# Attention on pairs of heads: VectorE and ScalarE work issued in written order by time behind each visit, and softmax transposes mostly in two PSUM banks of their own

## The chip, the core and the metric

The kernel runs on one NeuronCore of one Trainium2 chip. The metric is device time in microseconds (us) of one execution. The kernel before took 1141.73 us (median of 3 runs, 1139.65 to 1144.34). Its profiled execution took 1142.61 us, of which the span from the first to the last instruction is 1140.8 us.

The engines are named as the profile names them: PE is TensorE's matmul row and PEld its weight loads, DVE is VectorE, ACT is ScalarE, POOL is GpSimd, and SP is the engine that issues most transfers. L414 is line 414 of the kernel before.

## The reference

One layer on 1024 tokens of width 1024. Only the first third matters here:

```python
hn = rmsnorm(h, norm_mix_g[i])
z = hn @ w_in[i]                       # 512 columns for pooling, then q, k, v of 8 heads of 64
...
o = chunk_attention(q, k, v, rel_bias[i])
h = h + jnp.concatenate([a, o], axis=-1) @ w_out[i]
```

Attention works on chunks of 64 tokens; each sees itself and the 8 chunks before it, with a bias by clipped distance per head. A gated MLP with a causal convolution and a gated embedding follow; the change doesn't touch them.

## The kernel before, in words

Every product is made of three matmuls on a high and a low part of each operand (`mm3`, L136: high by high, high by low, low by high). So each matrix that enters a product is split first: ScalarE copies it to the rounded high part, and VectorE subtracts that from the source to give the low part (`split`, L142; ScalarE's half is L143, VectorE's L144).

**The attention stage** (L311 to L644) walks over 28 visits, `u` = 0 to 27, and a closing visit 28. The four groups of seven visits belong to the four pairs of heads. A visit takes one pair of heads and one tile of 128 query tokens (t = 2 to 7; the first visit of a pair takes t = 0 and 1 together). TensorE runs in the order in which the code is written. In a visit it does, in this order:

1. `probs_t(u-1)` (L380): transposes the finished softmax of the visit before, 64x64 blocks, up to 10 key tiles for the two heads, 20 matmuls (L395).
2. `scores(u)` (L357): the scores of this visit, 12 matmuls with up to 320 columns (L370), into PSUM banks 4 to 7, columns 0 to 320. The even banks belong to the first head, the odd ones to the second.
3. Filler: steps of a generator `rest()` (L587), which holds the projections for the other pairs of heads: q and k of pairs 1 and 2, the second half of v, q and k of pair 3, then the pooling columns. One step (a fill) is three matmuls of 512 columns, or six of 256 for v. A table (`fill_room`, L89) says how many fills each visit gets, 168 in all. The accumulating banks are 0 and 1 in turn, 8 fills to a bank (4 for v).
4. `values(u-1)` (L418), in every second visit: probabilities times v, 8 to 24 matmuls (L433, L434), into that one of banks 0 and 1 that isn't accumulating.

VectorE and ScalarE serve this. **Softmax** (L339): VectorE adds the bias and takes the row extreme (the reduction, L343 and L347), ScalarE exponentiates (L348), VectorE takes the reciprocal (L349), and the scaling is done by VectorE for the first head (L353) and by ScalarE for the second (L351). **Probabilities** (`probs_out`, L408): ScalarE copies the transposes out as high part (L413), VectorE forms the low part (L414). **Outputs**: ScalarE and VectorE fold the two halves of the output (L439, L440). **Banks**: a finished projection is taken out by VectorE (`qk_out` L279, `u_out` L517) or by both engines (`v_out` L274, L275). **Weights**: the next block of weights is loaded by SP and split (L454, L143, L144). **Lay**: q and k of the next pair are split (`lay`, L283). **Bias**: the table of the next heads is loaded and turned in sign by ScalarE (`load_bias`, L332, L335).

On these two engines a scheduler chose the order before: the code gives softmax, probabilities, outputs and bank clearing a raised priority (`tc.high_priority(AHEAD)`), and what is ready by the scheduler's reckoning is put in. The transposes of a visit with four or five key tiles lie in banks 4 to 7 from column 320 (key tiles 0 to 2 of each head) and in banks 2 and 3 (the rest), so that each head needs two copies per engine.

Of the kernel before, what the change touches and what calls it, by code (L numbers as in the profile page):

```python
# [64 lines left out]
FILL = 168  # L65
BASE = 6.0
# [14 lines left out]


def window_keys(u):

    t = UNITS[u][1][-1] if 0 <= u < NU else 0
    return min(t + 1, 6) if t % 2 else 0


def fill_room():  # L89


    vec_t, pe_t = [], []
    for u in range(NU):
        vec_t.append(BASE + 0.2 * (key_tiles(u) + key_tiles(u - 1)) + 0.25 * window_keys(u - 1))
        pe_t.append(0.4 + 0.18 * key_tiles(u) + 0.11 * key_tiles(u - 1) + 0.48 * window_keys(u - 1))
    lo, hi = 0.0, 10.0
    for _ in range(60):
        m = (lo + hi) / 2
        room = [max(0.0, m * v - p) / 0.68 for v, p in zip(vec_t, pe_t)]
        lo, hi = (m, hi) if sum(room) < FILL else (lo, m)  # L100
    return room


def trunk(tc, xT, pT, vecs, w_qk0, w_in, w_v, bias, counts, pool_w, w_out, w_up, w_down,
# [4 lines left out]
    with tc.tile_pool(name="sb", bufs=1) as sb, \  # L109
# [159 lines left out]
        def v_out(t, half, ps):  # L269
# [4 lines left out]
            act.activation(hi, pv, AF.Copy, scale=s)  # L274
            dve.scalar_tensor_tensor(lo, pv, s, rv(hi), ALU.mult, ALU.subtract)  # L275
# [5 lines left out]
        laid = set()  # L281

        def lay(c, x, h):  # L283

            laid.add((c, x, h))
            z = slice(h * 512, (h + 1) * 512)
            src = qk32[x][:, z]
            if x:
                hi, lo = [a[:, z] for a in K[c % 2]]
                return [lambda: act.activation(hi, src, AF.Copy),  # L290
                        lambda: dve.tensor_tensor(lo, src, rv(hi), ALU.subtract)]
            hi, lo = [a[:, z] for a in Q]
            return [lambda: act.activation(hi, src, AF.Copy, scale=-0.125),
                    lambda: dve.scalar_tensor_tensor(lo, src, -0.125, rv(hi), ALU.mult, ALU.subtract)]
# [37 lines left out]
        def load_bias(h):  # L332
            b = biasb[h % 3]
            sp.dma_start(b, bias[h])
            act.activation(b, b, AF.Copy, scale=-1.0)  # L335
            pool.memset(b[0:64, 576:640], BIG)
            pool.memset(b[64:128, 0:64], BIG)

        def softmax(x, b, ps, S, s_):  # L339

            n = S.shape[-1]
            if len(ps.shape) == 3:
                dve.tensor_tensor_reduce(  # L343
                    S.rearrange("p (a b) -> p a b", a=2), ps,
                    b.rearrange("p (a b) -> p a b", a=2), 1.0, BIG, ALU.add, ALU.min, s_[:, 0:1])
            else:
                dve.tensor_tensor_reduce(S, ps, b, 1.0, BIG, ALU.add, ALU.min, s_[:, 0:1])  # L347
            act.activation(S, S, AF.Exp, bias=s_[:, 0:1], scale=-1.0, accum_out=s_[:, 1:2])  # L348
            dve.reciprocal(s_[:, 2:3], s_[:, 1:2])  # L349
            if x:  # L350
                act.activation(S, S, AF.Copy, scale=s_[:, 2:3])  # L351
            else:
                dve.tensor_scalar(S, S, s_[:, 2:3], None, ALU.mult)  # L353
# [26 lines left out]
        def probs_t(u):  # L380
# [4 lines left out]
            def place(x, m):  # L385
                if total < 4:
                    return (6, 320 + HD * m) if x else (2, HD * m)
                return (4 + 2 * x, 320 + HD * m) if m < 3 else (2, P * x + HD * (m - 3))

            todo = []  # L390
            for x in range(2):
# [6 lines left out]
                for t in ts:  # L398
                    nk = min(t + 1, BANDT)
                    i0 = max(0, t - 4) - (t // 2 * 2 - 4)  # L400
                    parts = [(0, nk)] if total < 4 else [(0, 3), (3, nk)]
                    for a, b in parts:
                        bank, col = place(x, m + a)
                        todo.append((x, t % 2 * P, i0 + a, i0 + b, PS[:, bank:bank + 2, col:col + HD * (b - a)]))
# [3 lines left out]
        def probs_out(todo):  # L408
            for x, q, a, b, ps in todo:
                src = ps.rearrange("p a (k q) -> p a k q", q=HD)  # L410
                hi, lo = [PT[x][:, y, a:b, q:q + P].rearrange("p k (a q) -> p a k q", a=2) for y in range(2)]
                with tc.high_priority(AHEAD):
                    act.activation(hi, src, AF.Copy)  # L413
                    dve.tensor_tensor(lo, src, rv(hi), ALU.subtract)  # L414

        credit = 0.0

        def values(u):  # L418
# [5 lines left out]
            while c_ >= 2 and len(v_ready) < 2 * w + 2 or u < NU - 1 and at[0] < 2.0:  # L424
                next(fill)
                credit -= 1
            ks = list(range(max(0, 2 * w - 4), 2 * w + 2))
            for j in range(2):
                pt = PT[j]
                O = PS[:, (bankn[0] + 1) % 2, 256 * j:256 * j + 256]  # L430
                for n_, k in enumerate(ks):
                    idx = k - (2 * w - 4)
                    pe.matmul(O, V[:, k, 2 * c_ + j], pt[:, 0, idx], start=n_ == 0, stop=False)  # L433
                    pe.matmul(O, V[:, k, 2 * c_ + j], pt[:, 1, idx], start=False, stop=n_ == len(ks) - 1)  # L434
            for j in range(2):
                O = PS[:, (bankn[0] + 1) % 2, 256 * j:256 * j + 256]
                a, c = halves[j], halves[1 - j]
                with tc.high_priority(AHEAD):
                    act.activation(otmp[a], O[c], AF.Copy)  # L439
                    dve.tensor_tensor(o32[a, c_, w * 256:(w + 1) * 256], O[a], otmp[a], ALU.add)  # L440

# [6 lines left out]
        wvr = []  # L448

        def v_weights(z):  # L450
            for k in (slice(0, 2), slice(2, 4)):
                split(wvr[z][:, k], wv2[z][0][:, k], wv2[z][1][:, k])

        def weights(ct):  # L454
# [10 lines left out]
            for ks in (slice(0, 4), slice(4, 8)):  # L465
                split(t[:, ks], hi[:, ks], lo[:, ks])

        def project(ct, evac, wait=None):
            weights(ct)
            hi, lo = ready[ct]  # L470
            behind = blocks_[blocks_.index(ct) + 1] if ct != blocks_[-1] else None
            for h in range(2):
                bankn[0] += 1
                bank = bankn[0] % 2
                for k in range(KT):
# [906 lines left out]
```

## Time and profile before

| what | value |
|---|---|
| profiled execution | 1142.61 us |
| span of that execution | 1140.8 us |
| median of 3 runs | 1141.73 us |
| PE busy | 1120.6 us, 98% of the span |
| DVE busy | 866.2 us, 76% |
| ACT busy | 591.0 us, 52% |
| mean granted TensorE clock | 0.996 |

In a table of windows the first number of a cell is busy time in that stretch and the number in brackets counts instructions; PEclk is the granted clock. In a table of waits a row says who waited for whom, then the total, the number of times, and the longest. In a timeline the first number is the start in the span, the second the duration, and square brackets hold the idle time just ahead and what ended it. In a table of groups the numbers behind the bar are the total busy time and the mean of one in nanoseconds.

### The profile page before, as it was taken

The page shows a single profiled execution, that of the slowest core. Times are in us where ns is not written, and L with a number is a line of the kernel's source. Part 1 is how long each engine was busy: PE and PEld are TensorE (multiplying, and loading weights), DVE is VectorE, ACT ScalarE, POOL GpSimd, SP SyncE. Part 2 cuts the span into 40 slices and gives each one's busy share as a digit, 9 for nine tenths or more (in the row PEclk, how much of TensorE's full clock was granted, in tenths as well). Part 3 has the DMA queues.
Part 4 walks back from the last instruction along what each step waited for, and adds up shares of the span by engine and source line. Part 5 has one row for each costly group of instructions (what it writes and reads, how often), then busy time and mean ns, then how long its engine had stood idle before and what let it go on. Part 6 is the DMA issues. An engine that isn't in the chain of part 4 may idle for free.

```text
span 1140.8 us, 16198 instructions
## 1 busy us (share of the span) xinstructions
PE 1120.6 (98%) x5914; PEld 936.7 (82%) x5914; DVE 866.2 (76%) x1532; ACT 591.0 (52%) x1076; POOL 142.6 (12%) x188
## 2 busy tenths in 40 slices
PE   9999999999999999999999999999999999999997
PEld 7987888878788888888888888888888888888887
DVE  8576658678747887787787888787877789986845
ACT  8466667664744554444434444444444445564634
POOL 0000000056003200030102110211021102000000
PEclk9999999999999999999999999999999999999999
DMA  8101001105600055476557655765576556520003
GB/s 280 41 32 56 25 24 56 31 20 181 193 15 19 23 156 164 121 161 160 141 148 153 154 156 148 154 153 155 147 154 153 155 148 121 157 93 19 1 29 119
DMA packets 64879, 125.91 MB, mean 110 GB/s; under 512 B 7328, under 2 KB 8736, under 8 KB 64800
## 3 DMA queue, kind: packets, MB, share of 16 engines
q1 hardware_dynamic: 50688, 99.38, 26.8%
q0 software_dynamic: 13824, 25.17, 13.9%
q8 instruction: 46, 0.75, 0.3%
q14 instruction: 33, 0.27, 0.1%
q10 hardware_dynamic: 288, 0.33, 0.1%
HBM read 110.18 MB, written 14.68 MB: 109 GB/s over the span
## 4 chain that ended last, share of the span: by engine, by line
PE 83%; DVE 8%; ACT 5%; issue 2%; DMA 1%; POOL 1%; DVEq 0%; POOLq 0%; ACTq 0%; SPq 0%
PE PS L138 26%; PE PS L139 26%; PE PS L140 25%; DVE R L144 2%; PE PS L434 1%; PE PS L433 1%; ACT F L348 1%; ACT R L143 1%; PE PS L370 1%; DVE F L343 1%; ACT B L413 1%; DMA F<-in_w_out 1%; PE PS L395 1%; DVE B L414 1%; DVE F L440 1%
## 5 line engine op out<-in xcount | busy, mean ns | idle before, releaser
L138 PE MATMUL PS<-R 128*128 128x512 f32 (+1 forms) x1104 | 425.7, 386 | 1.7 <-ACT F L858 0.6
L139 PE MATMUL PS<-R 128*128 128x512 f32 (+1 forms) x1104 | 422.4, 383 | 0.0
L140 PE MATMUL PS<-R 128*128 128x512 f32 (+1 forms) x1104 | 422.2, 382 | 0.0
L138 PEld LDWEIGHTS PS<-R 128*128 128x128 f32 x1104 | 208.0, 188 | 45.1 <-ACT F L858 1.8
L140 PEld LDWEIGHTS PS<-R 128*128 128x128 f32 x1104 | 207.9, 188 | 40.5
L139 PEld LDWEIGHTS PS<-R 128*128 128x128 f32 x1104 | 208.1, 188 | 40.2 <-DVE R L248 1.3
L143 ACT ACTIVATE R<-F 128x512 fp32r<-128x512 f32 (+2 forms) x235 | 146.8, 636 | 179.6 <-PE PS L139 87.0
L144 DVE TENSOR_TENSOR R<-F,R 128x512 fp32r<-128x512 f32 (+2 forms) x235 | 162.7, 703 | 45.6 <-ACT R L143 42.4
L771 DVE TENSOR_TENSOR F<-F 128x512 f32<-128x512 f32 x88 | 60.5, 688 | 49.4 <-DMA F<-in_w_up 48.1
L1081 DVE TENSOR_TENSOR F<-F,PS 128x512 f32<-128x512 f32 x140 | 92.5, 681 | 6.2 <-PE PS L140 6.0
L143 ACT ACTIVATE BQ<-RW 128x512 fp32r<-128x512 f32 x90 | 52.6, 622 | 77.3 <-PE PS L139 73.3
L1024 POOL DMA_DIRECT2D RW<-Yd x56 | 49.5, 884 | 262.4 <-DMA RW<-Yd 199.1
L1024 POOL DMA_DIRECT2D RW<-in_w_down x40 | 36.1, 950 | 230.6 <-DMA RW<-in_w_down 194.0
L144 DVE TENSOR_TENSOR BQ<-RW,BQ 128x512 fp32r<-128x512 f32 x90 | 59.1, 685 | 2.5 <-PE PS L139 1.3
L414 DVE TENSOR_TENSOR B<-PS,B 128x384 fp32r<-128x384 f32 (+2 forms) x104 | 45.8, 460 | 15.8 <-ACT B L413 15.0
L348 ACT ACTIVATE F<-F,small 128x640 f32<-128x640 f32 (+4 forms) x64 | 44.3, 693 | 23.0 <-DVE small L343 20.0
L139 PE MATMUL PS<-BQ 128*128 128x512 f32 x140 | 54.6, 390 | 0.1
L140 PE MATMUL PS<-BQ 128*128 128x512 f32 x140 | 54.5, 390 | 0.0
L139 PE MATMUL PS<-R,BQ 128*128 128x512 f32 x140 | 54.5, 390 | 0.0
L138 PE MATMUL PS<-BQ 128*128 128x512 f32 x140 | 54.5, 389 | 0.0
L140 PE MATMUL PS<-R,BQ 128*128 128x512 f32 x140 | 54.5, 389 | 0.0
L138 PE MATMUL PS<-R,BQ 128*128 128x512 f32 x140 | 54.5, 389 | 0.0
(175 smaller groups left out, 1683.5 us busy)
## 6 DMA issues: line engine op xcount, KB each, us to landing
F<-in_w_up SPq DMA_DIRECT2D x91, 256.0 KB, 4.2
RW<-Yd SPq DMA_DIRECT2D x60, 256.0 KB, 3.7
RW<-Yd POOLq DMA_DIRECT2D x56, 256.0 KB, 5.0
RW<-in_w_down SPq DMA_DIRECT2D x50, 256.0 KB, 2.9
RW<-in_w_down POOLq DMA_DIRECT2D x40, 256.0 KB, 6.1
Yd<-F SPq DMA_DIRECT2D x40, 256.0 KB, 3.5
F<-in_w_in SPq DMA_DIRECT2D x10, 512.0 KB, 3.5
F<-in_xT SPq DMA_DIRECT2D x16, 256.0 KB, 5.8
```

The lines of the kernel that those rows point to most:

```text
L138: pe.matmul(ps, ahi, bhi, start=first, stop=False, skip_group_check=more)
L139: pe.matmul(ps, ahi, blo, start=False, stop=False, skip_group_check=more)
L140: pe.matmul(ps, alo, bhi, start=False, stop=last, skip_group_check=more)
L143: both = (act.activation(hi, src, AF.Copy), dve.tensor_tensor(lo, src, rv(hi), ALU.subtract))
L144: dve.tensor_tensor(lo, src, rv(hi), ALU.subtract))
L343: dve.tensor_tensor_reduce(S.rearrange("p (a b) -> p a b", a=2), ps, b.rearrange("p (a b) -> p a b", a=2), 1.0, BIG, ALU.add, ALU.min, s_[ ...
L348: act.activation(S, S, AF.Exp, bias=s_[:, 0:1], scale=-1.0, accum_out=s_[:, 1:2])
L370: pe.matmul(PS[:, places[x][y], 0:wide], q[halves[x], t * P:(t + 1) * P], k[halves[x], ki + y * wide:ki + (y + 1) * wide], start=i == 0, s ...
L414: dve.tensor_tensor(lo, src, rv(hi), ALU.subtract)
L771: return dve.tensor_tensor(rawu[to], rawu[a], rawu[b], op)
L1024: pool.dma_start(t, src, accum_op=ALU.add)
L1081: dve.tensor_tensor(t, t, PS[:, 4 + d], ALU.subtract if n in (1, 5) else ALU.add)
```

## The change

Three things change, and no arithmetic.

1. **Order on VectorE and ScalarE.** In the 29 visits both engines now run in written order. Each piece of work is pushed with a time in us behind the start of the visit (`push`), and `flush` writes out all that is pending in the order of these times. A flush comes ahead of `values`, at the end of the visit's fills, and where a bank or weights that are still pending are needed. The bias table is turned at the end of the seventh and of the second visit of a pair, not where it is loaded.
2. **Fill.** `fill_room` goes; a row of seven numbers (`ROOM`) serves each pair. `project_v` gives control back once ahead of its first matmul, and the visit's loop ends when the generator does so.
3. **Banks.** The transposes of both heads are numbered in one row; the first eight go to banks 2 and 3, the ninth and tenth to banks 6 and 7 from column 384.

```diff
-FILL = 168
-BASE = 6.0
+ROOM = (5.5, 5.5, 6, 5.5, 7, 5.5, 7)
+STEP = 0.68
...
+        pending, now, owed = [], [0.0], set()
+
+        def push(t, *fns):
+            for n, fn in enumerate(fns):
+                pending.append((t + 0.8 * n, len(pending), fn))
+
+        def flush():
+            todo = sorted(pending, key=lambda p: p[:2])
+            pending.clear()
+            owed.clear()
+            for _, _, fn in todo:
+                fn()
...
+                push(1.0 + 0.8 * z, least)
+                push(1.9 + 0.85 * z, lambda S=S, s_=s_: act.activation(
+                    S, S, AF.Exp, bias=s_[:, 0:1], scale=-1.0, accum_out=s_[:, 1:2]))
+                push(3.4 + 0.35 * z, lambda s_=s_: dve.reciprocal(s_[:, 2:3], s_[:, 1:2]))
+                push(3.9 + 0.1 * z, scaled)
...
             def place(x, m):
-                if total < 4:
-                    return (6, 320 + HD * m) if x else (2, HD * m)
-                return (4 + 2 * x, 320 + HD * m) if m < 3 else (2, P * x + HD * (m - 3))
+                n = total * x + m
+                return (2, HD * n) if n < 8 else (6, 384 + HD * (n - 8))
...
-                with tc.high_priority(AHEAD):
-                    act.activation(hi, src, AF.Copy)
-                    dve.tensor_tensor(lo, src, rv(hi), ALU.subtract)
+                push(0.9 if bank > 3 else 0.3 * n, lambda hi=hi, src=src: act.activation(hi, src, AF.Copy))
+                push(2.6 + 0.3 * n, lambda lo=lo, src=src, hi=hi: dve.tensor_tensor(lo, src, rv(hi), ALU.subtract))
+                n += bank < 4
...
-            while c_ >= 2 and len(v_ready) < 2 * w + 2 or u < NU - 1 and at[0] < 2.0:
+            while c_ >= 2 and len(v_ready) < 2 * w + 2 or u < NU - 1 and at[0] < 1.3:
                 next(fill)
                 credit -= 1
+                now[0] += STEP
+            flush()
...
+        def split_later(ct, parts):
+            t = max(5.2, now[0] + 0.4)
+            for i, (src, hi, lo) in enumerate(parts):
...
+                push(t + 0.7 * i, lambda src=src, hi=hi: act.activation(hi, src, AF.Copy), low)
...
         def project(ct, evac, wait=None):
             weights(ct)
+            if ct not in there:
+                flush()
...
         def project_v():
             v_weights(1)
+            yield False
+            flush()
...
                 def evac(h, ps, x=x):
-                    qk_out(x, h, ps)
+                    push(now[0] + 0.2, lambda: qk_out(x, h, ps))
...
                 lay_due(u)
-                credit += room[u]
-                while credit >= 1 and next(fill, True) is not False:
+                credit += ROOM[u % PER]
+                now[0] = 1.25
+                while credit >= 1:
+                    now[0] += STEP
                     credit -= 1
+                    if next(fill, True) is False:
+                        break
                     lay_due(u)
...
+            flush()
+            if u:
+                values(u - 1)
+            if turns and (u % PER == PER - 1 or u % PER == 1):
+                turns.pop(0)()
+            run_later(LATER)
...
+        with tc.manual_schedule(engines={mybir.EngineType.Activation, mybir.EngineType.DVE}):
+            for u in range(NU + 1):
+                unit(u)
```

How the rows of the built programs move is shown at three places. Lines of the changed kernel have other numbers; what they are is said each time.

**Place 1: PE at visit 11** (second pair, t = 5). Before, the row with 20 transposes (L395) and the 12 scores (L370) is followed by the fills of v (L138 to L140):

```order
L434 MATMUL PS<-B,R 128x256
L395 MATMUL PS<-ident,F 128x64 x20
L370 MATMUL PS<-R 128x320 x12
L138 MATMUL PS<-B,R 128x256
L139 MATMUL PS<-B,R 128x256
L140 MATMUL PS<-B,R 128x256
```

Now (L406 transposes, L382 scores, L449 the last of `values`, L117 and L118 a fill):

```order
L449 MATMUL PS<-B,R 128x256
L406 MATMUL PS<-ident,F 128x64 x20
L382 MATMUL PS<-R 128x320 x12
L406 MATMUL PS<-ident,F 128x64 x20
L382 MATMUL PS<-R 128x320 x12
L117 MATMUL PS<-R 128x256
L118 MATMUL PS<-R 128x256
```

Visit 11 has lost all its fills; they stand in visit 12, behind the second row of scores. The second row of transposes needs the softmax of the scores just ahead of it.

**Place 2: ACT around visits 15 and 16** (third pair, t = 2 and 3), where the weights of the block behind v are split. Before, L143 on R and B are these splits, L348 the exponentials of visit 15, L351 its scaling:

```order
L143 ACTIVATE R<-F 128x512
L348 ACTIVATE F,small<-F,small 128x384
L274 ACTIVATE R<-PS,small 128x4x64
L143 ACTIVATE R<-F 128x512
L348 ACTIVATE F,small<-F,small 128x384
L143 ACTIVATE R<-F 128x512
L143 ACTIVATE B<-F 128x512
L351 ACTIVATE F<-F,small 128x384
```

Now (L362 the exponentials of visit 16, L253 a piece of v, L358 the scaling, L473 the splits):

```order
L425 ACTIVATE B<-PS 128x2x3x64 x2
L362 ACTIVATE F,small<-F,small 128x512 x2
L253 ACTIVATE R<-PS,small 128x4x64
L358 ACTIVATE F<-F,small 128x512
L473 ACTIVATE R<-F 128x512 x2
L473 ACTIVATE B<-F 128x512 x2
```

The splits moved from between the exponentials of visit 15 to behind the scaling of visit 16. On PE the block that needs them begins in visit 16, after four products of v: the first matmul of the block waits for the first of these splits.

**Place 3: DVE at visit 5** (first pair, t = 6). Before, L343 is the reduction, L279 clears a projection's bank, L349 the reciprocal, L414 the low parts, L353 the scaling, L440 the outputs of `values`:

```order
L343 ISA F,small<-PS,F 128x640
L343 ISA small 128x1
L279 TENSOR_TENSOR F<-PS,F 128x512
L349 RECIPROCAL small<-small 128x1
L144 TENSOR_TENSOR B<-F,B 128x512
L414 TENSOR_TENSOR B<-PS,B 128x2x3x64 x2
L353 TENSOR_SCALAR F<-F,small 128x640
```

Now (L350 reduction, L426 low parts, L364 reciprocals, L360 scaling, L262 clearing of the bank, L470 splits, L455 outputs):

```order
L350 ISA F,small<-PS,F 128x640
L350 ISA small 128x1
L426 TENSOR_TENSOR B<-PS,B 128x2x5x64
L426 TENSOR_TENSOR B<-PS,B 128x2x3x64
L426 TENSOR_TENSOR B<-PS,B 128x2x2x64
L364 RECIPROCAL small<-small 128x1 x2
L360 TENSOR_SCALAR F<-F,small 128x640
L262 TENSOR_TENSOR F<-PS,F 128x512
L470 TENSOR_TENSOR B<-F,B 128x512 x2
L455 TENSOR_TENSOR F<-PS,F 64x256 x2
```

The bank is cleared last of the softmax work and no longer right behind the reductions. `values` of this visit writes into that bank. There are three low parts in place of four.

More of the change, by code (lines that the diff above doesn't have):

```diff
@@ L434, in values @@
                     pe.matmul(O, V[:, k, 2 * c_ + j], pt[:, 1, idx], start=False, stop=n_ == len(ks) - 1)
+            Os = [PS[:, (bankn[0] + 1) % 2, 256 * j:256 * j + 256] for j in range(2)]
             for j in range(2):
[L436 to L440, printed above, removed]
+                act.activation(otmp[halves[j]], Os[j][halves[1 - j]], AF.Copy)
+            for j in range(2):
+                a = halves[j]
+                dve.tensor_tensor(o32[a, c_, w * 256:(w + 1) * 256], Os[j][a], otmp[a], ALU.add)
         nw = [0]
@@ L483, in project @@
                         yield False
-                    run_later(len(later))
-                with tc.high_priority(AHEAD):
-                    evac(h, PS[:, bank])
+                evac(h, PS[:, bank])
+                owed.add(bank)
         def project_v():
             v_weights(1)
+            yield False
+            flush()
             for t in range(NTOK):
@@ L501, in project_v @@
                         yield True
-                with tc.high_priority(AHEAD):
-                    v_out(t, 1, PS[:, bank, 0:256])
+                push(now[0] + 0.2, *v_outs(t, 1, PS[:, bank, 0:256]))
+                owed.add(bank)
                 v_ready.append(t)
@@ L599, in trunk @@
         fill = rest()
-        room = fill_room()
         def lay_due(u):
@@ L606, in lay_due, with unit @@
                     qk_ready.remove((c, x, h))
-                    later.extend(lay(c, x, h))
+                    push(max(5.2, now[0] + 0.4), *lay(c, x, h))
         for h in range(3):
-            load_bias(h)
-        for u in range(NU + 1):
+            load_bias(h)()
+        def unit(u):
+            nonlocal credit
+            now[0] = 0.0
             if u < NU:
```

126 lines of the change are left out of this document (63 added, 63 removed).

## The prediction

> **What bounds the kernel now.** I read the page's head and its chain first, then the stages, then what PE waits for.
>
> ```profile
> span 1140.8 us, 16198 instructions
> PE 1120.6 (98%) x5914; PEld 936.7 (82%) x5914; DVE 866.2 (76%) x1532; ACT 591.0 (52%) x1076; POOL 142.6 (12%) x188
> PE 83%; DVE 8%; ACT 5%; issue 2%; DMA 1%; POOL 1%; DVEq 0%; POOLq 0%; ACTq 0%; SPq 0%
> ```
>
> PE is the bound: 98% busy, and 83% of the chain that ended last. The change adds no PE work and takes none away (the same fills, transposes and scores), so only PE's idle time and its clock can move. Where is the idle time?
>
> ```profile
> 0.00:54.00 54.00, 52.52 (x322) 46.06 (x322) 35.87 (x60) 34.64 (x58) 3.50 (x16) 1.00 0.49 166
> 54.00:86.00 32.00, 31.91 (x238) 26.10 (x239) 23.93 (x73) 21.21 (x55) 0.00 (x0) 1.00 0.11 34
> 86.00:262.00 176.00, 166.07 (x1393) 141.93 (x1390) 123.49 (x338) 117.62 (x283) 21.76 (x42) 0.99 0.13 40
> 262.00:310.00 48.00, 47.01 (x232) 38.15 (x231) 39.43 (x77) 30.84 (x55) 12.29 (x19) 1.00 0.61 186
> ```
>
> The columns are the stretch, its length, and the busy time of PE, PEld, DVE, ACT and POOL. Attention's visits run from 54 to 262 us. PE idles 0.1 us there up to 86 us and 9.9 us after it: 10.0 us in all. The next question is what it waits for.
>
> ```profile
> PE PS L395 <- ACT F L351: 4.9, 8, 1.0
> PE PS L395 <- DVE F L353: 2.0, 3, 1.0
> PE PS L138 <- DVE F L440: 1.2, 2, 0.7
> PE PS L434 <- DVE B L414: 0.9, 2, 0.5
> PE PS L433 <- DVE R L275: 0.5, 1, 0.5
> ```
>
> The transposes (L395) wait for the scaling of the second head on ScalarE and of the first on VectorE, 6.9 us; the rest is outputs, low parts and one v tile. The two worst places, with the clock:
>
> ```profile
> 102.32 0.53 PE L395 MATMUL PS<-ident,F 64*128 64x64 f32 x10 [0.68 <-DVE F L353]
> 103.83 0.52 PE L395 MATMUL PS<-ident,F 64*128 64x64 f32 x10 [0.98 <-ACT F L351]
> 158.94 0.74 ACT L335 ACTIVATE F<-F 128x640 f32<-128x640 f32 x1 [0.64 <-DMA F<-in_bias]
> 159.16 0.53 PE L395 MATMUL PS<-ident,F 64*128 64x64 f32 x10 [0.99 <-DVE F L353]
> 160.45 0.53 PE L395 MATMUL PS<-ident,F 64*128 64x64 f32 x10 [0.76 <-ACT F L351]
> 101.20:104.20 3.00, 1.34 (x24) 0.78 (x23) 1.83 (x5) 2.48 (x5) 0.29 (x2) 1.00 0.28 102
> 104.20:107.60 3.40, 3.40 (x23) 2.79 (x20) 2.74 (x14) 2.91 (x11) 0.29 (x2) 0.52 0.00 0
> ```
>
> At 102 and 159 us ScalarE stood at the bias turn (L335) for a load, with the scaling queued behind. After the first of these the granted clock was 0.52 for 3.4 us: 1.6 us lost. Idle and clock make 11.6 us, all that a perfect order could win: 1.0%.
>
> **The change, part by part.** I first take away the whole 11.6 us and then put back what the new order makes PE wait. For that I need one visit with five key tiles, and the lengths of the pieces.
>
> ```profile
> 241.31 0.84 PE L395 MATMUL PS<-ident,F 64*128 64x64 f32 x20
> 241.97 1.13 PE L370 MATMUL PS<-R 64*128 64x320 f32 x12
> 243.02 0.50 PE L138 MATMUL PS<-R,B 128*128 128x512 f32 x1
> 244.43 0.82 DVE L343 CUSTOM_DVE_ANT_0 F<-PS,F 128x640 f32<-128x640 f32 x1
> 245.17 0.82 DVE L343 CUSTOM_DVE_ANT_0 F<-PS,F 128x640 f32<-128x640 f32 x1
> 248.01 0.53 PE L395 MATMUL PS<-ident,F 64*128 64x64 f32 x10
> 248.03 0.83 ACT L351 ACTIVATE F<-F,small 128x640 f32<-128x640 f32 x1 [0.26 <-DVE small L349]
> ```
> ```profile
> L414 DVE TENSOR_TENSOR B<-PS,B 128x384 fp32r<-128x384 f32 x44 | 23.0, 551 | 0.5
> L414 DVE TENSOR_TENSOR B<-PS,B 128x256 fp32r<-128x256 f32 x38 | 15.8, 423 | 9.9 <-ACT B L413 9.6
> L440 DVE TENSOR_TENSOR F<-PS,F 64x256 f32<-64x256 f32 x30 | 12.6, 422 | 29.9 <-ACT F L439 29.4
> L349 DVE RECIPROCAL small<-small 128x1 f32<-128x1 f32 x62 | 9.7, 158 | 3.6 <-ACT F L348 3.3
> L353 DVE TENSOR_SCALAR F<-F,small 128x640 f32<-128x640 f32 x15 | 8.7, 580 | 0.3
> L279 DVE TENSOR_TENSOR F<-PS,F 128x512 f32<-128x512 f32 x12 | 8.1, 678 | 1.1 <-PE PS L140 1.1
> L343 DVE CUSTOM_DVE_ANT_0 F<-PS,F 128x512 f32<-128x512 f32 x8 | 5.2, 689 | 0.1
> ```
> ```profile
> L348 ACT ACTIVATE F<-F,small 128x640 f32<-128x640 f32 x31 | 25.7, 829 | 15.8 <-DVE small L343 15.8
> L413 ACT ACTIVATE B<-PS 128x256 fp32r<-128x256 f32 x38 | 14.1, 382 | 9.1 <-DVE B L414 7.4 <-PE PS L395 1.2
> L439 ACT ACTIVATE F<-PS 64x256 f32<-64x256 f32 x30 | 11.3, 378 | 19.7 <-PE PS L434 15.1 <-DVE F L440 4.3
> L143 ACT ACTIVATE R<-F 128x512 fp32r<-128x512 f32 x17 | 10.6, 626 | 5.8 <-PE PS L434 3.6 <-PE PS L139 2.0
> L348 ACT ACTIVATE F<-F,small 128x512 f32<-128x512 f32 x8 | 5.7, 718 | 4.4 <-DVE small L343 4.2
> L274 ACT ACTIVATE R<-PS,small 128x256 fp32r<-128x256 f32 x9 | 4.2, 464 | 0.8 <-PE PS L140 0.8
> ```
>
> PE in that visit, counted from its transposes: the scores end at 1.8, the fills start at 1.7, and seven fills end at 6.7 (0.71 each); six would end at 6.0, five at 5.3.
>
> *A regular visit in the new order.* The ninth and tenth transposes lie in banks 6 and 7 with the scores. In the built program their copy waits for the scores, and the first head's reduction waits for that copy: 1.8 + 0.38 = 2.2. Two reductions, 0.74 apart, end at 3.75. Three low parts of 640 (0.81, an estimate by the slope from 256 to 384), 384 and 256 wide take 1.8: 5.5. The exponentials (0.83 and about 0.1 for their read) run from 3.0 to 4.9 beside them. Two reciprocals and the scaling: 5.5 + 0.2 + 0.58 = 6.25; ScalarE's scaling (0.83) ends at 6.5. Before, that ended at 248.86, 7.55 into the visit. So a visit with seven fills waits for nothing, with 0.2 to 0.4 us to spare. The merged copies also save 24 instructions per engine, about 0.17 us each (0.42 less 256 times the slope), off the path. The bias turn costs nothing: it stands behind the scaling, and its load has the visit as cover; if that cover went, it would be the 1 to 2 us of 102 us again. On SP's queue only weights that are due visits later stand behind this load. POOL's two clearings of the table follow the turn and hold the second head's reduction in visits 7, 14 and 21 by some 0.3, where four short reductions leave room; that lies within the bounds of the third term below. What is late next is in the four terms below.
>
> *Visit 11: no cover.* Its fills are gone, so PE idles from 1.8 until the scaling is done. A clearing of a bank (0.68) stands there between reductions and low parts: 6.25 + 0.68 = 6.9, or 5.1 us; issue overlaps a little, so **5.0** (4.3 to 5.6).
>
> *Visit 16: the splits behind the scaling.* PE has 1.3 us of transposes and scores and twelve short matmuls of v (1.4 us), then needs the new weights at 2.7. ScalarE gets there thus: outputs and VectorE's two additions to 1.65, reductions of 512 (0.69) to 3.0, two exponentials of 0.72 and their 0.1 read from 2.4 to 4.1, a piece of v 0.46, the scaling (0.7, an estimate from 0.83 at 640) and the split 0.63, with a little overlap: 5.7. The first low part adds 0.2. **3.2** (2.0 to 4.0); before, the splits stood a visit earlier and PE didn't wait.
>
> *Banks cleared late.* In visits 5, 14, 15 and 21 `values` writes to a bank whose clearing now stands behind the scaling. Visit 5: cleared at 6.25 + 0.68 = 6.9, PE there at 6.0: 0.9. Visits 14 and 15 the same with a v tile: 0.9 each. In visit 21, with four short reductions, three reciprocals and two scalings ahead, the bank is clear at about 7.0, and PE is there after five fills at 5.2: 1.8. Three more by 0.2. **5.1** (2.5 to 8).
>
> *Transposes still late, outputs late.* Visit 18 has six fills and a split (0.63) ahead of the third copy: 6.8 against 6.0. Visits 4 and 20 have a clearing between the reciprocals: 6.9 against 6.7, and q's low part in 21 is 0.3 late. **1.5** (0.5 to 4). In visits 13, 15 and 23 the first fill goes into the bank that `values` has just used; two output copies and two additions (0.38, 0.42) end at 1.65 against 1.7, 1.1 and 1.3, and splits ahead of them add some: **1.3** (0.5 to 2).
>
> *Clock.* The stall of 5.0 is longer than the 1.7 us of gaps that halved the clock at 104 us, that of 3.2 too; but 1.75 us of gaps at 159 us didn't. I take 1.6 for the first and 0.9 for the second: **2.5** (0.9 to 3.4). [...]
>
> Sum: 5.0 + 3.2 + 5.1 + 1.5 + 1.3 + 2.5 = 18.6, less 11.6: 7.0 us slower. The profiled execution (1142.6) becomes 1149.6; it stands 0.9 above the median, so the median becomes **1148.7**. The low ends add up to 10.7, the high ends to 27: 1141 to 1157.
>
> **Rivals.**
>
> *Not slower: the two stalls are all.* If VectorE issues each piece some 0.1 us sooner than the rows' durations (they overlap at their ends), the late clearings and transposes vanish and only visits 11 and 16 and the clock are left: 10.7 for 11.6, or 1140.8. For it: reductions of 0.82 start 0.74 apart. Against: nine pieces gain 0.7 us, which covers visits 4, 18 and 20, not visit 21. The point: visits 5 and 18 have to find their work done 6.0 after the transposes.
>
> *Slower still: the third copy holds up every five-key visit.* ScalarE first does outputs (two of 0.38) and two copies; if they end at 2.6 and not at 1.8, the whole chain moves to 7.0 and 16 visits wait 0.3 to 0.5: 7 us more, 1156. For it: 7.4 us of ScalarE's idle time ahead of the 256-wide copies was spent waiting on VectorE's low part in the same bank. [...]
>
> *Given back.* The stage from 262 us has VectorE busy for 39.4 of 48 us and PE idle for 1.0. If VectorE is ahead when PE arrives late, at most that 1.0 comes back: 1147.5.
>
> *Not what it says.* The rows of the built program show the order moved, so this has no chance of its own.
>
> **How the numbers follow.** Forecast 0.50 (1145 to 1153), not slower 0.25, slower still 0.17, given back 0.08. A measurement of this kernel tells about 0.5% (5.7 us) from no change: slower starts at 1147.4, faster at 1136.0. Slower takes three quarters of the forecast, all of slower still, and half of given back: 0.57. Faster needs the first rival with both stalls at half: 0.05. Same: 0.38. The range runs from the first rival, 1139.5, to the second, 1156.
>
> **What would show it.** In the changed profile: one gap of about 5 us ahead of transposes near 140 us with a granted clock near 0.5 behind it; one of about 3 us ahead of a 512-wide fill some 40 us later, released by the split on ScalarE; waits of L433's successor on the clearing of a bank, 1 to 2 us; no gap at the bias turn; PE's transposes elsewhere without waits. It is wrong if visit 11 costs under 4 us, if the regular visits wait at each step, or if PE's work itself changed.

## The result, and the profile after

The changed kernel took 1154.91 us (median of 4 runs, 1153.92 to 1155.19); the kernel before took 1141.8 us beside it. The ratio is 1.0112, with a 95% interval of 1.0091 to 1.0134: 13.1 us slower, where 7.0 were forecast: above the forecast's own 1145 to 1153, and within the range of all cases (1139.5 to 1156). The profiled execution took 1155.19 us. Its page head and its chain:

```profile
span 1153.4 us, 16190 instructions
PE 1122.8 (97%) x5914; PEld 939.5 (81%) x5914; DVE 861.3 (75%) x1508; ACT 588.4 (51%) x1052; POOL 144.4 (13%) x188
PE 87%; DVE 5%; ACT 3%; POOL 2%; issue 2%; POOLq 0%; DVEq 0%; ACTq 0%
```

VectorE and ScalarE have less to do than before (861.3 and 588.4 us, against 866.2 and 591.0). The span grew by 12.6 us: PE's busy time by 2.2, its idle time by the other 10.4. The table of windows shows where, with the columns as before, and below it three short stretches with their granted clock (the number behind POOL):

```profile
54.00:86.00 32.00, 32.00 (x259) 26.29 (x257) 23.39 (x69) 22.82 (x55) 0.00 (x0) 1.00 0.10 34
86.00:262.00 176.00, 164.48 (x1362) 140.74 (x1359) 114.57 (x312) 114.00 (x261) 16.58 (x34) 0.97 0.10 34
262.00:310.00 48.00, 38.48 (x188) 31.73 (x187) 35.38 (x67) 20.66 (x36) 19.18 (x26) 0.89 0.49 154
134.80:140.20 5.40, 5.38 (x43) 5.05 (x44) 3.17 (x7) 3.71 (x9) 0.00 (x0) 0.50 0.28 97
181.10:184.50 3.40, 3.40 (x14) 2.26 (x14) 0.93 (x2) 0.00 (x0) 0.00 (x0) 0.51 0.64 224
285.90:290.30 4.40, 4.33 (x10) 3.46 (x11) 4.40 (x10) 0.58 (x1) 0.00 (x0) 0.50 0.92 298
```

Up to 262 us PE idles for 11.5 us, 1.5 more than before. From 262 to 310 us it idles for 9.5 us, where it was 1.0: most of the loss lies in the stage to which the prediction gave 1.0 us at most, and as a gain. What PE waited for between 54 and 330 us (total, times, longest), and the three long gaps in the timeline:

```profile
PE PS L117 <- DVE F L455: 9.4, 1, 9.4
PE PS L406 <- DVE F L360: 5.5, 2, 4.9
PE PS L117 <- ACT R L473: 2.6, 1, 2.6
PE PS L117 <- ACT B L425: 1.3, 2, 0.7
PE PS L448 <- DVE F L262: 1.1, 2, 0.6
PE PS L117 <- DVE R L254: 0.5, 1, 0.5
```
```profile
134.82 1.33 PE L406 MATMUL PS<-ident,F 64*128 64x64 f32 x20 [4.94 <-DVE F L360]
179.56 0.50 PE L117 MATMUL PS<-R 128*128 128x512 f32 x1 [2.62 <-ACT R L473]
285.97 0.76 PE L117 MATMUL PS<-R,B 128*128 128x512 f32 x1 [9.38 <-DVE F L455]
```

The first two are visits 11 and 16, as forecast. The third isn't in the prediction. PE has done the last matmuls of `values` and needs the bank that VectorE's last outputs (L455) still read. VectorE's queue at that place, then GpSimd's (L547 is the clearing of group 3's bank, L560 a step of pooling on either engine, L123 the low part of a split):

```profile
263.25 0.69 DVE L547 TENSOR_TENSOR F<-PS,F 128x512 f32<-128x512 f32 x1
...
274.36 0.68 DVE L470 TENSOR_TENSOR R<-F,R 128x512 fp32r<-128x512 f32 x1
281.27 0.44 DVE L560 TENSOR_TENSOR F<-F 128x271 f32<-128x271 f32 x1 [6.23 <-POOL F L560]
281.63 3.42 DVE L123 TENSOR_TENSOR R<-F,R 128x512 fp32r<-128x512 f32 x4
284.97 0.85 DVE L455 TENSOR_TENSOR F<-PS,F 64x256 f32<-64x256 f32 x2
```
```profile
264.07 3.00 POOL L560 TENSOR_TENSOR F<-F 128x271 f32<-128x271 f32 x4 [6.03 <-issue]
279.09 2.15 POOL L560 TENSOR_TENSOR F<-F 128x269 f32<-128x269 f32 x3
```

VectorE pools groups 0 and 1, GpSimd groups 2 and 3, and both use the temporaries `T1` and `T2`. VectorE's first step stands at the head of its queue for 6.23 us, until GpSimd's last steps of L560 are over, and the last outputs stand behind it. In the kernel before the rows of the clearing, of VectorE's first step, and of GpSimd's start read:

```profile
254.72 0.67 DVE L517 TENSOR_TENSOR F<-PS,F 128x512 f32<-128x512 f32 x1
...
272.96 0.45 DVE L529 TENSOR_TENSOR F<-F 128x271 f32<-128x271 f32 x1
```
```profile
255.52 3.85 POOL L529 TENSOR_TENSOR F<-F 128x271 f32<-128x271 f32 x4 [6.36 <-issue]
```

There GpSimd began 8.5 us earlier, and VectorE found the temporaries free. Why does GpSimd begin late? Fills per visit, counted in the built programs (group 3's last fill is number 160; with number 95 the weights behind v are split):

```
visit          11 12 13 14 15 16 17 18 19 20 21 22 23 24 25 26   sum up to 26
before          6  6  6  6  4  7  5  7  5  7  5  8  5  5  7  4   160
after           0 12  7  5  6  6  6  6  6  7  5  6  6  5  7  6   160
fill11          7  7  6  6  5  6  5  7  6  7  5  7  5  5  7  7   162
keep_credit     0 14  6  6  5  6  5  7  6  7  5  7  5  5  7  7   162
```

Fill 160 is the last of visit 26 before and after, and the generator hands a finished bank over only at the *next* fill. Before, the scheduler still put the clearing ahead of visit 27's reductions; in written order it stands behind them. In `fill11` (below) the clearing falls into visit 26. And in the changed kernel a loop that is told "no fill now" in visit 11 has already paid for one (`credit -= 1` ahead of `next(fill, True) is False`); before, a refused fill cost no credit.

### The profile page after: what moved, and what is told of

Its sections match the earlier page's. It is cut to its first block, busy times and chain, and to the rows that moved or that the text cites. A ratio compares the mean times of both kernels' runs of the same rounds, so it can differ in the third digit from the quotient of the medians.

```text
span 1153.4 us, 16190 instructions
## 1 busy us (share of the span) xinstructions
PE 1122.8 (97%) x5914; PEld 939.5 (81%) x5914; DVE 861.3 (75%) x1508; ACT 588.4 (51%) x1052; POOL 144.4 (13%) x188
## 4 chain that ended last, share of the span: by engine, by line
PE 87%; DVE 5%; ACT 3%; POOL 2%; issue 2%; POOLq 0%; DVEq 0%; ACTq 0%
PE PS L117 27%; PE PS L118 27%; PE PS L119 27%; DVE R L123 1%; PE PS L448 1%; PE PS L449 1%; PE PS L382 1%; ACT B L425 1%; POOL F L560 1%; PE PS L406 1%; DVE B L426 1%; DVE F L350 1%; ACT R L122 1%; ACT F L452 0%; POOL TB L891 0%
## 5 line engine op out<-in xcount | busy, mean ns | idle before, releaser
L117 PE MATMUL PS<-R 128*128 128x512 f32 (+1 forms) x1104 | 426.5, 386 | 5.7 <-ACT R L473 2.6
L118 PE MATMUL PS<-R 128*128 128x512 f32 (+1 forms) x1104 | 422.5, 383 | 0.0
L117 PEld LDWEIGHTS PS<-R 128*128 128x128 f32 x1104 | 208.5, 189 | 50.5 <-ACT R L473 2.8
L118 PEld LDWEIGHTS PS<-R 128*128 128x128 f32 x1104 | 208.7, 189 | 39.5 <-DVE R L227 0.2
L122 ACT ACTIVATE R<-F 128x512 fp32r<-128x512 f32 (+2 forms) x221 | 138.0, 637 | 186.0 <-PE PS L118 78.8
L123 DVE TENSOR_TENSOR R<-F,R 128x512 fp32r<-128x512 f32 (+2 forms) x221 | 152.4, 701 | 45.0 <-ACT R L122 41.8
L123 DVE TENSOR_TENSOR BQ<-RW,BQ 128x512 fp32r<-128x512 f32 x90 | 59.0, 683 | 2.6 <-PE PS L118 1.7
L118 PE MATMUL PS<-BQ 128*128 128x512 f32 x140 | 54.6, 390 | 0.1
L117 PE MATMUL PS<-R,BQ 128*128 128x512 f32 x140 | 54.5, 389 | 0.0
L118 PE MATMUL PS<-R,BQ 128*128 128x512 f32 x140 | 54.5, 389 | 0.0
L117 PE MATMUL PS<-BQ 128*128 128x512 f32 x140 | 54.5, 389 | 0.0
L952 ACT ACTIVATE F<-F,vec 128x1024 f32<-128x1024 f32 (+1 forms) x25 | 28.6, 1143 | 47.9 <-DVE F L927 43.3
L362 ACT ACTIVATE F<-F,small 128x640 f32<-128x640 f32 (+4 forms) x64 | 44.0, 691 | 16.8 <-DVE small L350 15.1
```

The costliest lines, as they stand in the source:

```text
L117: pe.matmul(ps, ahi, bhi, start=first, stop=False, skip_group_check=more)
L118: pe.matmul(ps, ahi, blo, start=False, stop=False, skip_group_check=more)
L122: both = (act.activation(hi, src, AF.Copy), dve.tensor_tensor(lo, src, rv(hi), ALU.subtract))
L123: dve.tensor_tensor(lo, src, rv(hi), ALU.subtract))
L362: push(1.9 + 0.85 * z, lambda S=S, s_=s_: act.activation(S, S, AF.Exp, bias=s_[:, 0:1], scale=-1.0, accum_out=s_[:, 1:2]))
L952: act.activation(y, Gb[:, 2 + a:2 + b], AF.Identity, bias=vec[:, C_CB + fi:C_CB + fi + 1], scale=cw(2))
```

## The experiments

All times are medians, each beside a kernel before of 1141.2 to 1142.0 us.

**The tail.** Two edits that take away VectorE's wait in different ways. `own_t`:

```diff
-        T2 = f(55.3125, 272)
+        T2, T3, T4 = f(55.3125, 272), f(57.5, 272), f(58.5625, 272)
...
-                src, dst, m, lo_ = u, T1, 1, 0
+                src, ta, tb, m, lo_ = u, T1 if g >= 2 else T3, T2 if g >= 2 else T4, 1, 0; dst = ta
...
-                    src, dst = dst, (T2 if dst is T1 else T1)
+                    src, dst = dst, (tb if dst is ta else ta)
```

> The kernel after, with temporaries of their own for VectorE's pooling (groups 0 and 1), at the place of the third bias table, which is not used any more by then; GpSimd's pooling keeps the old ones. Nothing moves on any engine. Theory (shared buffers: VectorE's first pooling step waits 6.2 us for GpSimd's late chain, and the last outputs queue behind it): that wait is gone; the splits behind it still wait for ScalarE until about 280, so PE resumes near 281 instead of 286, 5 us earlier, and the half clock behind the gap gets 0 to 2 us shorter: 1147.5 to 1150 us against 1154.9. Rival (everything simply arrives late there, VectorE is full): the gap of 9.4 us stays within 1.5 us and the time is 1153.5 to 1156.

`early_g3` calls `evac` behind the last fill of group 3, ahead of its `yield`:

```diff
-                    yield True
+                    yield (ct, h, k) == (3, 1, KT - 1) and evac(h, PS[:, bank]) or True
...
-                evac(h, PS[:, bank])
+                (ct, h) != (3, 1) and evac(h, PS[:, bank])
```

> The kernel after, with one clearing of a bank moved: the second half of pooling group 3 is read from its bank behind its last fill, in visit 26, not at the next fill in visit 27. VectorE is idle there for 1.8 us. The temporaries stay shared. Theory of the shared buffers: GpSimd's chain starts near 258 instead of 264 us and ends near 275, so VectorE's first pooling step waits 0.5 us or less, and the time falls as with temporaries of its own: 1147.5 to 1150 us. Rival (VectorE is full at the end whatever GpSimd does): GpSimd starts earlier, the gap stays, 1153.5 to 1156. Third theory (separate memory is what helps, not the order): no gain here but one with temporaries of its own.

Measured: 1149.7 us (1.0083, 1.0068 to 1.0098) and 1149.55 us (1.0081, 1.0066 to 1.0097): 5.2 and 5.4 us gained, as the theory of the shared temporaries has it. Moving GpSimd's start does as much as other memory, so the third theory falls too. PE's wait for the last outputs in the two:

```profile
PE PS L117 <- DVE F L455: 6.0, 1, 6.0
```
```profile
PE PS L117 <- DVE F L455: 4.6, 1, 4.6
```

Some of the gap stays. In `early_g3` VectorE's first pooling step still waits 1.33 us, where 0.5 or less was expected. In `own_t` VectorE goes on at once, but ScalarE's output copies (L452) stand behind splits that wait for a load of output weights:

```profile
277.97 1.26 ACT L122 ACTIVATE R<-F 128x512 fp32r<-128x512 f32 x2 [4.20 <-DMA F<-in_w_out]
280.35 0.77 ACT L452 ACTIVATE F<-PS 64x256 f32<-64x256 f32 x2
```

**Visit 16.** `split16` gives the new block's splits the time 1.0, ahead of the exponentials, instead of `max(5.2, now[0] + 0.4)`.

> The kernel after, with one pair of splits moved: the weights of visit 16's new block are split ahead of the exponentials, not behind the scaling. Theory (the wait of 2.6 us and 1.7 us of half clock behind it are the cost): PE waits 0.7 us or less there, the chain of visit 16 ends 1.3 us later but before visit 17 needs it: 1150.5 to 1152.5 us against 1154.9. Rival (ScalarE is the bound of visit 16 in any order, and a late softmax stalls visit 17 instead): a gap of 1 to 3 us ahead of visit 17's transposes, and 1153.5 to 1156.

Measured: 1150.4 us (1.0088, 1.0070 to 1.0106), 4.5 us gained, at the theory's edge. The wait for the split is gone from the list, and no transposes of visit 17 wait.

**Visit 11.** `fill11` splits v's weights at time 1.0 and refuses no fill:

```diff
-            v_weights(1)
-            yield False
+            v_weights(1, 1.0)
             flush()
```

> The kernel after, with the fills of visit 11 back: the second half of v's weights is split ahead of the exponentials of that visit, and its projection goes on in the same visit. Theory (the stall and its half clock are what that edit costs): the gap of 4.9 us shrinks to 1 us or less (the first two fills need only the first half of the weights) and the 2.7 us of half clock behind it go: 1147 to 1150.5 us against 1154.9. Rival (visit 11's idle time is slack that later visits use: with fills in it, VectorE and ScalarE are late in visits 12 to 16): gaps of 1 to 2 us appear ahead of transposes there, and the time is 1152 to 1155.

Measured: 1137.7 us (0.9969, 0.9957 to 0.9982): 17.2 us gained, more than twice what either theory allowed, and 0.3% under the kernel before. PE's longest waits between 54 and 330 us:

```profile
PE PS L117 <- ACT B L122: 1.5, 1, 1.5
PE PS L448 <- DVE F L262: 1.5, 2, 0.9
PE PS L118 <- DVE B L470: 1.1, 2, 0.8
```

With visit 11's gap, those of visit 16 and of the tail have gone too. Two causes were possible: the stall leaves VectorE and ScalarE behind, or the lost credit moves the end of each later block. The table of fills shows how to part them: `keep_credit` keeps the empty visit and saves the credit, `fill11_less` fills the visit and loses the credit.

```diff
 (keep_credit)
-                    credit -= 1
                     if next(fill, True) is False:
                         break
+                    credit -= 1
 (fill11_less, on top of fill11)
-                credit += ROOM[u % PER]
+                credit += ROOM[u % PER] - (u == 11)
```

> The kernel after, with visit 11 still empty, but the credit for a fill no longer taken when the fill is refused. Visit 12 then has 14 fills instead of 12, and from visit 13 on every visit has the fills that it has in fill11 (group 3's last fill in visit 26, the new block's splits in visit 15). Theory (the refused fill shifts the whole schedule by a fill or two, and this shift makes the waits of visit 16 and of the end): only visit 11's gap of 4.9 us and its 2.7 us of half clock stay over fill11's 1137.7: 1145 us (1143 to 1147). Rival (the stall itself leaves ScalarE and VectorE behind, and this makes the two later waits): they stay, 1152 to 1156.

> fill11 (visit 11 has its fills) with one fill's credit taken away in visit 11: from visit 13 on every visit has the fills of the kernel after. Theory (the shift): visit 11 has no long gap, but the wait of 2.6 us at visit 16 and the one of 9.4 us at the end are back with their half clocks: 1154.9 less 7.6, 1147 us (1145 to 1150). Rival (without the stall ahead of them nothing is late): 1136 to 1140.

Measured: 1141.12 us (0.9991, 0.9979 to 1.0004) and 1149.1 us (1.0067, 1.0049 to 1.0085). `keep_credit` came out below the 1143 to 1147 that the theory gave, so the stall costs less than that; its rival (1152 to 1156) is far off.

| | later visits as in `fill11` | later visits as after | difference |
|---|---|---|---|
| visit 11 filled | 1137.7 | 1149.1 | 11.4 |
| visit 11 empty | 1141.1 | 1154.9 | 13.8 |
| difference | 3.4 | 5.8 | |

The two long waits follow the schedule and not the stall. First `keep_credit`, whose list has visit 11 at the top and neither of the others, then `fill11_less`:

```profile
PE PS L406 <- DVE F L360: 5.6, 3, 4.9
PE PS L448 <- DVE F L262: 1.4, 2, 0.9
PE PS L117 <- ACT B L122: 1.4, 1, 1.4
```
```profile
PE PS L117 <- DVE F L455: 9.4, 1, 9.4
PE PS L117 <- ACT R L473: 2.6, 1, 2.6
```

They are back at 9.4 and 2.6, to the tenth, though visit 11 has no long stall. In the schedule of `fill11`, fill 95 is the last of visit 15 (up to there 95 fills, not 94), so the splits are written a visit earlier, and fill 160 lies inside visit 26. `fill11_more` asks whether that schedule is a lucky one: one credit more in visit 11.

> fill11 with one fill's credit more in visit 11 (eight fills there, and each later block ends one fill earlier). Theory (the late waits come from a block's end falling just behind the end of a visit, and one fill earlier is on the safe side): no wait over 1 us at visit 16 or at the end, 1136 to 1140. Rival (fill11's schedule is a lucky one, every shift of one fill costs): over 1142.

Measured: 1136.12 us (0.9947, 0.9933 to 0.9960). One credit more is safe here, one less costs 11.4 us.

**The banks.** `fill11_old_banks` puts the old `place` and `parts` back into `fill11`; `before_new_banks` gives the kernel before the new ones.

> fill11 with the transposes put in the banks of the kernel before: the first three key tiles of each head in the scores' banks, the rest in two of their own (four copies per visit, not three). Theory: two 384-wide copies (0.5 us each), not one of 256, then stand between the scores and the reductions, the chain of each five-key visit ends some 0.6 us later, and PE waits 0.1 to 0.5 us in some 15 visits: 1140 to 1147 against fill11's 1137.7. Rival (the visits have spare time, the banks make no difference): 1136.5 to 1139.

> The kernel before with the new places of the transposes alone; its scheduler orders VectorE and ScalarE as it sees fit. Theory (fewer copies that wait for the scores; ScalarE's 7.4 us of waiting on low parts in its bank go): the late scalings of before get shorter: 1136.5 to 1140.5 against 1141.2. Rival (the scheduler puts the wide low parts between the two reductions, and the second head is late): 1142 to 1148.

Measured: 1143.8 us (1.0016, 1.0006 to 1.0025), 6.1 above `fill11`; and 1136.72 us (0.9961, 0.9947 to 0.9976), 5.2 under before. The banks alone are a gain of 5 to 6 us under either order. With the old ones the small waits grow; here the transposes (now L407), the clearings, and a split for the output weights at the end:

```profile
PE PS L448 <- DVE F L262: 3.0, 3, 1.5
PE PS L407 <- DVE F L360: 2.9, 7, 1.1
PE PS L117 <- ACT B L122: 2.3, 1, 2.3
PE PS L117 <- DVE R L254: 1.7, 2, 1.0
```

The theory of `fill11_old_banks` shows in VectorE's 640-wide reductions, which wait for the copies out of the scores' banks: 18.1 us with the old places, 10.0 with the new, so 8.1 us over 16 visits (group of `fill11_old_banks`, then of `fill11`, from 54 to 310 us):

```profile
L350 DVE CUSTOM_DVE_ANT_0 F<-PS,F 128x640 f32<-128x640 f32 x32 | 25.1, 822 | 18.1 <-ACT B L425 18.1
```
```profile
L350 DVE CUSTOM_DVE_ANT_0 F<-PS,F 128x640 f32<-128x640 f32 x32 | 25.1, 822 | 12.5 <-ACT B L425 10.0 <-PE PS L382 2.4
```

The reason that I gave for `before_new_banks` does not hold, though. ScalarE still waits for low parts under the scheduler: ahead of the 384-wide copies 12.0 us, more than the 8.2 ahead of the 256-wide ones before, from 54 to 310 us (group of `before_new_banks`, then the same one of `fill11`; in the same stretch):

```profile
L413 ACT ACTIVATE B<-PS 128x384 fp32r<-128x384 f32 x24 | 11.8, 490 | 12.4 <-DVE B L414 12.0
```
```profile
L425 ACT ACTIVATE B<-PS 128x384 fp32r<-128x384 f32 x24 | 11.2, 484 | 0.0
```

What shrank in `before_new_banks` is PE's own waiting from 54 to 310 us (11.0 us before, 8.0 here), and the half clock behind the gaps at 102 us (0.52 for 3.4 us before) is not there: from 86 to 131 us the granted clock is 1.00, where it was 0.96. Which of the fewer copies did it stays open.

**A version that beats both.** `best` is `fill11` without the second load and split of v's weights. `best2` evicts v's tiles earlier as well, `before_best` is `before_new_banks` without that second load.

```diff
-                    if (h, k) == (0, 2):
+                    if (h, k) == (0, 2) and ct != blocks_[-1]:
                         weights(behind)
 (best2 too)
-                push(now[0] + 0.2, *v_outs(t, 1, PS[:, bank, 0:256]))
+                push(now[0] - 0.6, *v_outs(t, 1, PS[:, bank, 0:256]))
```

> fill11 without the second load and split of v's weights that both kernels make during the last block (it is not used): four splits and two loads of 512 KB less near 258 to 265 us. Theory (output weights then land some 3 us earlier, and ScalarE and VectorE have 5 us less to do where PE waited 1.5 and 0.4 us for splits): 1134.5 to 1137 against fill11's 1137.7. Rival (the scheduler puts other work ahead of the last outputs, and PE waits for those): 1138 to 1141.

> The same, and v's tiles are evicted 0.8 us earlier in the order by time (ahead of the second reciprocal or of the third low part), so that the next tile or values find their bank clear. Theory (four waits of 0.3 to 0.5 us, 1.4 in all, go): 0.5 to 1.4 us under the kernel without that. Rival (the eviction now waits for its own fills at the head of VectorE's or ScalarE's queue and holds the softmax up): 0 to 2 us over it.

> The kernel before with the new places of the transposes and without the second load and split of v's weights; its scheduler orders the rest. It tells what the written order itself is worth on top of the banks. Theory (the written order wins some 2 to 4 us of the 7 that this kernel still waits for late scalings and outputs): 1134.5 to 1136.5 here, and the written one with the same two edits 1 to 3 us below it. Rival (the order by itself wins nothing): the two within 1 us, or the written one above.

Measured: `best` 1133.63 us (0.9925, 0.9912 to 0.9937), 8.4 us under before; `best2` 1135.73 (0.9942, 0.9929 to 0.9956); `before_best` 1137.73 (0.9961, 0.9948 to 0.9975). `best` lies 4.1 us under the median of `fill11`, and a little under the range expected. Its profiled execution is only 1.8 us shorter than that of `fill11` (1133.78 against 1135.59, the fastest of its eight), with 1.1 us less idle time from 54 to 310 us; what made the rest of the 4.1 is not shown.

The earlier eviction gains nothing, and the intervals of `best` and `best2` overlap. `values` now waits longer for v's low parts (in `best2`; it was 0.7, 2, 0.5):

```profile
PE PS L448 <- DVE R L254: 1.9, 2, 1.2
```

Other waits fall, and from 54 to 310 us PE idles 6.4 us in `best2` against 5.8 in `best`. Most of the other difference between the two profiles is one wait far behind attention (for L903, 1.8 us against 0.5), so that the rival's reason is not shown.

What is the written order worth on top of the banks? `best` lies 4.1 us under `before_best`, but `fill11` lies 1.0 above `before_new_banks`, the same pair with the second load. By the idle time from 54 to 310 us the order saves 2.7 us in the first pair (8.6 to 5.8) and 1.1 in the second (8.0 to 6.9). `before_best` itself missed its 1134.5 to 1136.5: under the scheduler the second load costs nothing that these runs show (1136.72 with it, 1137.73 without). With the old banks the written order loses 1.9 us (1143.8 against 1141.9). So the order gains, if at all, together with the new banks, and how much stays open between nothing and 4 us.

## Why the prediction was right in sign and 6 us short

By its steps:

- *The 11.6 us taken away*: right. No gap stands at the bias turn. At the end of visit 15 it follows the outputs, with no wait for its load:

```profile
174.07 0.77 ACT L452 ACTIVATE F<-PS 64x256 f32<-64x256 f32 x2 [1.83 <-PE PS L449]
174.86 0.74 ACT L338 ACTIVATE F<-F 128x640 f32<-128x640 f32 x1
```

- *Visit 11, 5.0*: measured 4.94. What it is worth as a whole is 3.4 to 5.8 us by the table of four, since filling it costs 1.1 us of waits for the new low parts, and since the half clock behind the gap varies: it lasted from 133.3 to 140.2 us in the kernel after (granted clock 0.51), with PE back at work from 134.8 us on, and some 3.4 us in `own_t` and `early_g3`, whose programs are the same up to there (an estimate from the mean clock from 131 to 146 us: 0.89 in these two, 0.77 in the kernel after).
- *Visit 16, 3.2*: measured 2.62, and 4.5 with its half clock (0.51 for 3.4 us) by `split16`.
- *Banks cleared late, 5.1*: measured 1.6 (1.1 for L262 and 0.5 for v's low part). This term was too large by 3.5. Banks came clear earlier than I built them, and PE arrived later. In visit 21 the transposes began at 214.45; I had the bank clear 7.0 behind that and PE there at 5.2, and it was 6.4 (the end of L262) and 6.0 (220.93 less the wait of 0.52):

```profile
214.45 0.88 PE L406 MATMUL PS<-ident,F 64*128 64x64 f32 x20
...
220.93 0.39 PE L448 MATMUL PS<-B,R 128*128 128x256 f32 x1 [0.52 <-DVE F L262]
```
```profile
217.94 1.62 DVE L426 TENSOR_TENSOR B<-PS,B 128x640 fp32r<-128x640 f32 x3
...
220.19 0.68 DVE L262 TENSOR_TENSOR F<-PS,F 128x512 f32<-128x512 f32 x1
```

  The three low parts, for one, take 1.62 together where I had 1.8.
- *Transposes late, 1.5, and outputs late, 1.3*: measured 0.8 (5.5 less 4.94, and 0.2 for q's low part) and 1.3 (the two waits put down to L425, the copy that ScalarE makes right behind the outputs).
- *Clock, 2.5*: three half-clock stretches, 13.1 us of PE's work. By an estimate that costs between 2.2 us (the growth of PE's busy time) and 4.8 (half of 13.1, less half of the 3.4 of before). The third stretch belongs to the tail.
- **The step that failed** is the one on the stage from 262 us: "at most that 1.0 comes back". I read its 1.0 us of idle time as the most that could be won there, and priced nothing that could be lost. I had the rows of the fills in hand, but read from them only which visit stood empty, not in which visit each later block ends. The shared temporaries were in the code, and so was the fill ahead of which a bank is handed over.

Up to 262 us the sum was 16.1 for 11.5 us of measured idle time, 4.6 too much; the tail is 8.5 us of idle time more than I allowed; the busy time grew by 2.2 and not by 0.9. That makes 5.2 of the 5.6 us between the forecast and the profiled execution. That the time fell within the range is in part luck: the upper end stands for a rival that did not happen, and the term on the banks, too large by 3.5, hid part of the tail that no term held. Two figures of the prediction do not follow from its own sums: "given back" is 1148.7 less 1.0, so 1147.7 and not 1147.5, and the first rival's time is 1140.8, where the range starts at 1139.5. Neither changes the forecast.

Of the rivals, "not slower: the two stalls are all" was nearest on the visits themselves, though it left out the tail. "Slower still: the third copy holds up every five-key visit" is wrong: with two such copies, as before, the kernel is 6.1 us slower than with one.

## What to carry to other kernels

Where a generator of filler work is moved by a count, write down for both kernels in which visit each of its blocks *ends* and what starts from that end; a shift of one or two fills in the middle cost 11 to 14 us here, more than the 3 to 6 us of the stall itself. Before a stage is called harmless because nothing waits there, ask which in-order queue holds an instruction that depends on another engine's chain, and how much later that chain may start (here GpSimd began 8.5 us later, and VectorE stood 6.2 us for it). And a change made of several parts can lose as a whole while its parts win: here the banks were worth 5 to 6 us under either order, and one refused fill hid that. What the order adds on top lies between nothing and 4 us.

## What the runs showed of the hardware

**The length of a gap alone did not decide here whether half clock followed.** The same gap of 2.62 us in front of the same matmul was followed in the kernel after by a granted clock of 0.51, for 3.4 us from 1.5 us behind its end (second short stretch above), and in `fill11_less`, where PE resumed at 174.85 us, by 1.00:

```profile
172.20:174.90 2.70, 0.08 (x2) 0.05 (x1) 2.15 (x9) 2.70 (x8) 0.00 (x0) 1.00 0.00 0
174.90:178.30 3.40, 3.40 (x18) 2.28 (x20) 2.43 (x4) 1.47 (x3) 0.00 (x0) 1.00 0.23 66
178.30:181.70 3.40, 3.40 (x37) 2.87 (x34) 1.95 (x5) 2.16 (x5) 0.00 (x0) 1.00 0.71 242
```

In `own_t` the same gap (2.6 us) ended at 178.78 us (179.00 less the 0.22 us of PE's work since), and half clock began some 0.5 us behind it: an estimate from the granted clock, 1.00 from 176.9 to 179.0 us and 0.55 from 178.9 to 182.3. In `early_g3`, with a gap of 2.6 us too, the clock from 176 to 190 us was 0.88 on average, as in `own_t` and in the kernel after. Shorter gaps behaved alike: waits of 1.38 and 0.36 us for the output weights in `keep_credit`, the second ending at 290.5 us, were followed by half clock from 290.6 to 294.0 us (matmuls of 0.63 us, not 0.39; 0.96 on average from 262 to 310 us), and 1.51 and 0.36 us at the same place in `fill11` by none (0.39 us a matmul; 1.00). What decides, the moment of the gap or something else, these runs leave open.

**VectorE's splits took longer beside pooling on GpSimd: 1.135 us, against 0.68.** In `own_t` both work at once from 275 us on. VectorE's 512-wide low parts took 1.135 us each there (row of its groups from 275 to 280 us), and 0.68 in the kernel after, once GpSimd had ended (least, median, most in ns, from 285.9 us on):

```profile
L123 DVE TENSOR_TENSOR R<-F,R 128x512 fp32r<-128x512 f32 x4 | 4.3, 1135 | 0.0
```
```profile
L123 DVE TENSOR_TENSOR R<-F,R x7: 680/682/694, 285.9 to 299.2; 128x512 fp32r<-128x512 f32 x7
```

It cost `own_t` little, since VectorE then stood 1.47 us for ScalarE's output copies anyway. The splits, longer by 0.45 us, ran beside pooling steps that took 0.9 to 1.2 us each in that stretch; what holds them up there is not shown.
